# Warm-up on a tile of ones, and sums of squares behind the products, in the opening of an encoder layer

## The chip, the cores and the metric

The kernel runs on one core of a Trainium2 chip. The metric is the device time of one execution in microseconds (us), the median over timed runs. Before the change it is 1359.25 us (three runs, 1358.98 to 1361.77).

The core's engines each run their own queue of instructions in order: TensorE (PE, matmuls), VectorE (DVE), ScalarE (ACT), GpSimd (POOL) and SyncE (SP, which here only issues DMAs). They wait for one another through semaphores. A DMA that is to write into a buffer still in use stands at the head of its queue until the buffer is free, and what was queued after it stands too.

## The reference, cut to what matters

One layer of a bidirectional encoder: sequence 1024, model width 1024, fp32. Only the beginning matters here.

```python
cond = jax.nn.silu(c)
mod = cond @ w_ada[l] + b_ada[l]
sh1, sc1, g1, sh2, sc2, g2 = jnp.split(mod, 6, axis=-1)
h = modulate(rms_norm(x, norm_mix_g[l]), sh1, sc1)      # (x * rsqrt(mean(x*x)) * g) * (1 + sc1) + sh1
proj = h @ w_in[l]
q_a, k_a, v_a, qk_m, v_m, o_m, gates = jnp.split(proj, splits, axis=-1)
...                                                      # attention and mLSTM heads, output projection, SwiGLU
```

The sum of squares of each of the 1024 tokens is needed for the norm, but the norm is a factor per token and can be multiplied in after a projection.

## The kernel before

Everything is held transposed: x is eight tiles of 128 model rows by 1024 tokens (`x_t[k]`, k = 0 to 7), worked on in two halves of 512 tokens (n = 0, 1). A product in fp32 quality is made from three fast ones: both operands are split into a rounded high part and a remainder (`hh` and `hl` for the input, `whi` and `wlo` for weights), and `mm3` (line 311) issues high x high, high x low and low x high. ACT makes the high part, DVE or POOL the remainder. A plain fp32 matmul (the warm-up, the sums of squares) is two passes on PE.

**The opening.** While x and the first rows of w_ada arrive, DVE makes a column of `mod` from each ada tile (`ada_load`, line 565, 512 KB each, a tile ring of five; a8 to a15 give the scale sc1, a0 to a7 the shift). `z_steps` (line 570) scales x by sc1 and splits it, before the norm is known. PE then runs, for each k, the products of that k with three column tiles of w_in (f = 0, 1, 2) into six PSUM accumulators `acc0` (the loop at line 700). The weights come in pieces of four k: pieces 0 to 2 serve k = 0 to 3 and pieces 3 to 5 the rest; `split` (line 461) splits each after its DMA into a ring of three `wst` tiles.

**The sums of squares.** `square_steps` (line 547) has ACT square each half of each x_t. For k below `PES` (3) the square is a tile of `small()` (line 519, a ring of five) that PE adds up over the 128 rows with a matmul by `ones`, into `msp[n]` (line 704). From k = 3 on DVE adds the squares into `ssx`, and after k = 5 one more matmul per half adds that (line 720). In the old order the two sums of a k stand ahead of its products.

**After k = 5** `rstd_steps` (line 616) makes the reciprocal root of each half: a root on ACT and a scaled copy on DVE, a square on ACT, and two steps on DVE. Then `h_steps` (line 686), for each n and k, multiplies x by it (DVE), applies scale and shift (ACT, needs column k of the shift), rounds (ACT) and takes the remainder (POOL, or DVE for the first): new `hh` and `hl`. Up to three such chains are open at a time (`last[-3:-2]`). The three sums of `acc0` are read by DVE at the same time, times the root; when all six are read, the flag `late` is set, which the DVE steps of a4 to a7 wait for. After the eighth shift column ACT makes a diagonal matrix of the shift (`diagonal`, line 659). The next products (`acct`, from line 2128) use the new `hh` and `hl`, one k after the other.

**What sets the order.** All instructions are written out under a manual schedule by a planner (`Clock`, line 127) at the time the program is built. It keeps a clock for PE (`ck.t`), estimated free times of the other engines and a heap of events; a `chain` is a row of steps, each of which is written out when the planner's time reaches the end of the step before. `ck.need` moves PE's planned time to that of a flag, `ck.pe(d)` moves it by d, and both write out all events up to then. So a change of PE's planned time changes how instructions of other engines interleave in their queues, though the engines on the chip run by their real waits. The warm-up matmuls are not counted by the planner. The loads at the start follow a list (line 590: x tiles, ada tiles and weight pieces), and each is written out 5 us before the planner's DMA clock reaches it (line 604). Outside that list, three more weight pieces are loaded behind the products of k = 3:

```python
            z_read[k].set(ck, ck.t)
            if k == 3:
                for _ in range(3):
                    load_piece()
```

`load_piece` (line 488) issues the DMA on SP and appends the two steps of the split to ACT's and DVE's queues for the time when the planner has the piece arrive. Nearly all DMAs of the opening go through `dma` (line 316) to SP's queue.

## Time and profile before

| | us |
|---|---|
| timed runs, median of 3 | 1359.25 (1358.98 to 1361.77) |
| profiled execution, its own time | 1354.44 |
| profiled execution, span of its instructions | 1352.7 |
| PE busy | 1275.2 (94%) |
| DVE busy | 1053.8 (78%) |
| ACT busy | 710.0 (52%) |
| POOL busy | 533.6 (39%) |
| first PE instruction | 7.26 |
| warm-up matmuls (line 684) | 7.29 to 12.3 |

The times within the profile count from the span's first instruction. A row of a list gives start, duration, engine, line, operation, written and read tile by their names (buffer numbers left out), shape and count; a bracket gives the engine's idle time before it and what ended it. Line 98 is the wrapper through which all DVE, ACT and POOL steps are written out, so those steps are told apart by their tiles. Line 317 likewise stands for nearly all DMAs. PEld is the loading of the stationary operand, which overlaps the matmuls; matmuls are pipelined, so their spacing is read from starts, not from durations.

### The profile page before, as it was taken

How to read it: one execution, taken by the hardware profiler on the slowest of the kernel's cores; microseconds unless marked ns; L12 is line 12 of the kernel's file. 1: busy time of each engine (PE TensorE's matmuls, PEld its weight loads, DVE VectorE, ACT ScalarE, POOL GpSimd, SP SyncE). 2: the span in 40 equal slices, each digit the busy share in tenths (PEclk: the TensorE clock that was granted, in tenths of full speed). 3: DMA queues.
4: the chain of work that ended last, by engine and by line, in shares of the span. 5: the costliest groups of instructions: out<-in, count | busy, mean ns of one | idle time of the engine just before them, and what ended most of it. 6: DMA issues, size and time to landing. Idle time of an engine off the chain costs nothing.

```text
span 1352.7 us, 19570 instructions
## 1 busy us (share of the span) xinstructions
PE 1275.2 (94%) x6596; PEld 1072.6 (79%) x6596; DVE 1053.8 (78%) x1683; ACT 710.0 (52%) x1342; POOL 533.6 (39%) x454
## 2 busy tenths in 40 slices
PE   7898888899999989999999999999999999999997
PEld 5777767788778979788778788888888887788886
DVE  7936698976789847889888989876666655888886
ACT  6576366778577756455477522333232333554452
POOL 0352577655666523444125155555544530000002
PEclk9898999999999999999999999999999999999999
DMA  9444332233233226673553344423332258943324
GB/s 365 158 138 131 107 110 94 88 99 108 66 93 106 75 83 199 216 263 113 179 179 113 101 144 145 137 94 109 110 117 86 72 178 304 335 109 94 94 58 161
DMA packets 104468, 187.02 MB, mean 138 GB/s; under 512 B 11568, under 2 KB 33200, under 8 KB 104368
## 3 DMA queue, kind: packets, MB, share of 16 engines
q1 hardware_dynamic: 90976, 163.68, 38.0%
q10 hardware_dynamic: 13392, 22.10, 4.3%
q8 instruction: 52, 0.85, 0.2%
q14 instruction: 48, 0.39, 0.1%
HBM read 139.33 MB, written 42.73 MB: 135 GB/s over the span
## 4 chain that ended last, share of the span: by engine, by line
PE 61%; DVE 18%; issue 7%; DMA 5%; ACT 5%; POOL 3%; SPq 1%; DVEq 0%; ACTq 0%; POOLq 0%
PE acc L314 16%; PE acc L312 16%; PE acc L313 16%; DVE sst L98 3%; DVE x L98 2%; DVE y L98 2%; PE av L1210 2%; PE T L1191 2%; DVE PT L98 2%; PE S L1159 2%; SPq L317 1%; PE U L1917 1%; DVE wlo L98 1%; POOL wlo L98 1%; PE ni L2001 1%
## 5 line engine op out<-in xcount | busy, mean ns | idle before, releaser
L98 ACT ACTIVATE whi<-wst 128x512 fp32r<-128x512 f32 (+2 forms) x223 | 134.0, 606 | 141.7 <-PE acc L314 60.1
L98 POOL TENSOR_TENSOR wlo<-wst,whi 128x512 fp32r<-128x512 f32 (+1 forms) x83 | 129.6, 1566 | 178.3 <-ACT whi L98 127.4
L313 PE MATMUL acc<-x,whi 128*128 128x512 f32 x352 | 136.9, 389 | 0.0
L98 POOL TENSOR_SCALAR P<-P,sst 128x1024 f32<-128x1024 f32 x64 | 86.0, 1345 | 88.0 <-DVE sst L98 67.0
L98 DVE TENSOR_TENSOR wlo<-wst,whi 128x512 fp32r<-128x512 f32 (+2 forms) x140 | 93.2, 669 | 32.0 <-ACT whi L98 31.4
L312 PE MATMUL acc<-hh,whi 128*128 128x512 f32 x224 | 96.9, 432 | 6.2 <-ACT xp L98 4.7
L98 POOL TENSOR_TENSOR x<-x,ny 128x256 f32<-128x256 f32 (+1 forms) x8 | 8.3, 1066 | 234.7 <-DMA wst<-act_d1T 214.3
L98 POOL TENSOR_TENSOR wlo<-wr,whi 128x512 fp32r<-128x512 f32 x52 | 72.2, 1389 | 71.7 <-ACT whi L98 68.6
L314 PE MATMUL acc<-whi,wcl 128*128 128x512 f32 x244 | 95.3, 390 | 2.6 <-DVE wcl L98 2.6
L312 PE MATMUL acc<-whi,wch 128*128 128x512 f32 x244 | 95.2, 390 | 2.4 <-ACT wch L98 2.4
L98 ACT ACTIVATE P<-S,sst,colq 128x1024 f32<-128x1024 f32 x64 | 77.2, 1207 | 34.4 <-DVE sst L98 30.5
L313 PE MATMUL acc<-wlo,wch 128*128 128x512 f32 x244 | 94.9, 389 | 0.0
L98 DVE TENSOR_TENSOR PT<-T,PT 128x512 fp32r<-128x512 f32 x128 | 83.3, 681 | 9.5 <-ACT PT L98 9.3
L313 PE MATMUL acc<-hl,whi 128*128 128x512 f32 x224 | 90.4, 404 | 0.0
L314 PE MATMUL acc<-hh,wlo 128*128 128x512 f32 x224 | 90.3, 403 | 0.0
L98 ACT ACTIVATE whi<-wr 128x512 fp32r<-128x512 f32 x56 | 35.4, 632 | 100.0 <-DVE wr L98 48.3
L1191 PE MATMUL T<-ident,P 128*128 128x128 f32 x512 | 71.9, 278 | 16.0 <-DVE PT L98 10.9
L98 ACT ACTIVATE PT<-T 128x512 fp32r<-128x512 f32 x128 | 71.8, 597 | 27.7 <-PE T L1191 26.9
L98 DVE TENSOR_REDUCE sst<-S 128x1 f32<-128x1024 f32 x64 | 77.7, 1213 | 9.8 <-PE S L1159 9.5
L312 PE MATMUL acct<-whi,hh 128*128 128x256 f32 (+1 forms) x256 | 80.5, 314 | 4.6 <-ACT hh L98 3.2
L1191 PEld LDWEIGHTS T<-ident,P 128*128 128x128 f32 x512 | 58.4, 142 | 27.3 <-issue 10.6
L1210 PE MATMUL av<-PT,va 128*128 128x256 f32 x512 | 70.9, 285 | 7.1 <-DVE PT L98 7.0
(482 smaller groups left out, 3855.0 us busy)
## 6 DMA issues: line engine op xcount, KB each, us to landing
wr<-in_w_gu_dram SPq DMA_DIRECT2D x66, 256.0 KB, 2.8
ada<-in_w_ada_dram SPq DMA_DIRECT2D x64, 256.0 KB, 3.4
wd<-in_w_d_dram SPq DMA_DIRECT2D x22, 512.0 KB, 6.8
wst<-in_w_gu_dram SPq DMA_DIRECT2D x42, 256.0 KB, 3.0
wst<-act_d SPq DMA_DIRECT2D x33, 256.0 KB, 3.1
ada<-in_w_ada_dram SPq DMA_DIRECT2D x16, 512.0 KB, 6.9
wst<-in_w_o_dram SPq DMA_DIRECT2D x32, 256.0 KB, 3.5
act_d<-sg ACTq DMA_DIRECT2D x29, 256.0 KB, 2.0
```

Source lines behind the costliest of these rows:

```text
L98: return fn(*args, **kw)
L312: nc.tensor.matmul(acc, w[0], x[0], start=first, stop=False)
L313: nc.tensor.matmul(acc, w[0], x[1], start=False, stop=False)
L314: nc.tensor.matmul(acc, w[1], x[0], start=False, stop=last)
L317: (q or nc.sync).dma_start(dst, src)
L1159: nc.tensor.matmul(sp[:, halves(n)], qs[:, j * P:(j + 1) * P], k2[g][m][:, halves(n)], start=m == 0, stop=m == 1)
L1191: nc.tensor.transpose(tp[:, k], Pt[q][:, (4 * b + k) * P:(4 * b + k + 1) * P], ident)
L1210: nc.tensor.matmul(av, va[:, k, h // 4], PT[it][m][:, k], start=(k, m) == (0, 0), stop=(k, m) == (NJ - 1, 1))
L1917: nc.tensor.matmul(U, T[:, i], wv[:, i], start=True, stop=True)
L2001: nc.tensor.matmul(ni, x["q"][:, i * P:(i + 1) * P], H["Cs"][b][:, i4], start=True, stop=True)
```

## The change

Two edits. The warm-up becomes 34 matmuls of the tile `ones` by itself, 128 columns wide, into the first 128 columns of the same accumulator; they read no input. And the two sums of squares of k = 0, 1 and 2 are written out after that k's products rather than ahead of them; the waits of the planner (`ck.need`, `ck.pe`) move with them.

```diff
-WARM = 4
+WARM = 34
...
         for _ in range(WARM):
-            nc.tensor.matmul(acc0[0][0][0], ones, x_t[0][:, 0:HALF], start=True, stop=True)
+            nc.tensor.matmul(acc0[0][0][0][:, 0:P], ones, ones, start=True, stop=True)
...
         for k in range(KT):
-            if k < PES:
-                for n in range(NH):
-                    ck.need(sq_ok[k][n])
-                    nc.tensor.matmul(msp[n][0], ones, by_pe[k, n], start=k == 0, stop=False)
-                    ck.pe(0.86)
             for n in range(NH):
                 ck.need(z_ok[k][n])
                 for f in range(3):
                     mm3(acc0[f][n][0], weights([f, 3 + f], k, 4), (h_hi[k][:, halves(n)], h_lo[k][:, halves(n)]),
                         k == 0, k == KT - 1)
                     ck.pe(0.68)
+            if k < PES:
+                for n in range(NH):
+                    ck.need(sq_ok[k][n])
+                    nc.tensor.matmul(msp[n][0], ones, by_pe[k, n], start=k == 0, stop=False)
+                    ck.pe(0.86)
             z_read[k].set(ck, ck.t)
```

## The prediction

> **What bounds the kernel now.** I read the page first, then the time-ordered list of each engine over the opening, then busy time by stretch. Over the whole span TensorE (PE) is the bound:

> ```profile
> PE 1275.2 (94%) x6596; PEld 1072.6 (79%) x6596; DVE 1053.8 (78%) x1683; ACT 710.0 (52%) x1342; POOL 533.6 (39%) x454
> ```

> The change lies in the first 44 us, so that stretch has to be read by itself. PE's list there and shortly after (start, duration, engine, line, operation, in brackets the idle time before it and who ended it):

> ```profile
> 7.29 5.19 PE L684 MATMUL acc<-x,ones 128*128 128x512 f32 x8 [7.29 <-DMA x<-in_xT_dram]
> 12.31 1.88 PE L704 MATMUL ms<-sq,ones 128*128 128x512 f32 x4
> ...
> 18.18 1.88 PE L704 MATMUL ms<-sq,ones 128*128 128x512 f32 x4
> ...
> 24.00 1.88 PE L704 MATMUL ms<-sq,ones 128*128 128x512 f32 x4
> ...
> 29.81 0.39 PE L312 MATMUL acc<-hh,whi 128*128 128x512 f32 x1
> ...
> 53.41 0.39 PE L312 MATMUL acct<-whi,hh 128*128 128x272 f32 x1 [1.30 <-ACT hh L98]
> ...
> 56.54 0.60 PE L314 MATMUL acct<-whi,hl 128*128 128x272 f32 x1 [2.61 <-DVE hl L98]
> ...
> 72.15 0.39 PE L312 MATMUL acct<-whi,hh 128*128 128x272 f32 x1 [1.95 <-ACT hh L98]
> ...
> 73.50 0.39 PE L314 MATMUL acct<-whi,hl 128*128 128x272 f32 x1 [0.83 <-POOL hl L98]
> ```

> The list is to be read by its brackets. PE sits idle for 7.29 us until x0 has landed, then runs four warm-up matmuls (5.19), k=0's two sums of squares (L704), k=0's products, and so on; no row from there to 51.9 has an idle bracket. After that it waits four times, for ACT, DVE and GpSimd (POOL). What the other engines were doing meanwhile:

> ```profile
> 29.82:42.06 12.24, 12.24 (x55) 10.13 (x54) 12.18 (x23) 6.54 (x11) 0.00 (x0) 1.00 0.83 288
> 42.06:52.00 9.94, 9.94 (x41) 7.33 (x39) 9.94 (x18) 6.16 (x13) 0.00 (x0) 1.00 0.70 242
> ```

> The columns are the stretch's length, then busy time of PE, weight loads, DVE, ACT and POOL, the granted clock and the DMA. VectorE (DVE) is full too: 12.18 of 12.24 us and 9.94 of 9.94. The waits from 53 to 73 end on hh and hl, the rewritten inputs, whose first step is a product on DVE. So DVE's queue sets the end of the opening, and PE's arriving sooner is worth little as long as that queue has no hole.

> **Part 1, the warm-up.** Eight passes (four fp32 matmuls, two passes each) go, 68 passes of 128 columns come. They need only the tile of ones, which is set by 1.1 us. Their pace, from weight loads, one per pass:

> ```profile
> 9.98 0.34 PEld L684 LDWEIGHTS acc<-x,ones 128*128 128x128 f32 x1 [0.52 <-issue]
> 10.60 0.19 PEld L684 LDWEIGHTS acc<-x,ones 128*128 128x128 f32 x1 [0.28 <-issue]
> ...
> 97.03 1.75 PEld L784 LDWEIGHTS ms<-con,sqk 128*128 128x128 f32 x15 [0.24 <-issue]
> ```

> A load and the idle time before it are one pass of 512 columns: 0.34 + 0.52 = 0.86 us at 9.98, and 0.43 from 10.60 on (0.19 + 0.24 in its neighbours). The pace changes some 3.1 us after PE's start. 128 columns are a quarter: 0.21 slow, 0.107 fast; and the last row, fifteen short passes with a load each in 1.75 us, 0.11 a pass, shows that loading does not hold that pace up. So 3.1 us hold 15 slow passes, the other 53 take 5.7, and the warm-up ends near 1.1 + 3.1 + 5.7 = 9.9. That is the lower end. If each pass also paid its load of 0.19 in full, 68 x 0.19 + 3.1 + 1.1 puts the end at 17. I take 9.9, since the row of fifteen does the same thing. When can products start?

> ```profile
> 11.24 1.42 DVE L98 SCALAR_TENSOR_TENSOR hl<-x,sc,hh 128x512 fp32r<-128x512 f32 x2
> 12.57 1.29 DVE L98 TENSOR_TENSOR wlo<-wst,whi 128x512 fp32r<-128x512 f32 x2
> ```

> A product of k=2 takes (29.81 - 24.00 - 1.72) / 18 = 0.227. The first remainder hl of k=0 is there at 12, the last weight tile at 12.57 + 1.29 = 13.86. So the first half's nine products, which need them one by one, end near 14.2, and the other nine at 16.25. Before, they ended at 18.18: 1.93 sooner.

> **Part 2, the sums after the products.** Two sums are four passes of 0.43, 1.72. Before, k=0's filled the time in which the weights were being split; now they come behind the products. Counting on from 16.25: sums 17.97, k=1 22.05, sums 23.8, k=2 27.9, sums 29.61. At the start of k=3 the changed PE has done the same work at 29.61 as the old one at 29.82: a gain of 0.21, and L720 comes 0.21 sooner. DVE's full queue hides it; I count 0. Without that cover it is worth 0.21.

> The sums free the squares' tiles, a ring of five. The sixth square (k=2, second half) must wait for k=0's first sum, now done near 16.25 + 0.86 = 17.1:

> ```profile
> 17.26 0.62 ACT L98 ACTIVATE sq<-x 128x512 f32<-128x512 f32 x1
> ...
> 19.50 1.34 ACT L98 ACTIVATE hh<-x,sc 128x512 fp32r<-128x512 f32 x2 [0.36 <-DVE sc L98]
> ```

> It just fits: cost 0. If the warm-up ended at 17, k=0's products would end near 21.1 and this square would stand until 22, with hh of k=2 behind it on ScalarE (ACT) and hl behind that on DVE; ACT's idle 0.36 taken off, some 4.4 would reach DVE: the upper bound of this part.

> **Part 3, the order.** The planner in the kernel writes the instructions out by a clock of its own. That clock decides their order, and I use it for nothing else. It counts 0.86 for a sum and 0.68 for three products. In the old plan k=0's sums hid in the wait for the first split; now every sum adds to PE's planned time. The products of k=1 and k=2 begin at the same planned moments as before (16.90 and 22.70), where sums used to go first; those of k=3 begin 2 x 0.86 later, 28.50 against 26.78, and end at 32.58 instead of 30.86. Right there three weight pieces are loaded (lines 713 to 715). Loads of ada come in the plan every 1.456 (512 KB at the planner's 360 GB/s): a3 at 29.65, a4 at 31.10, a5 at 32.56. So the pieces, which stood ahead of a4, now fall behind a5, by 0.02. The queue of SyncE (SP), which issues in order:

> ```profile
> 21.22 13.09 SPq L317 DMA_DIRECT2D ada<-in_w_ada_dram  x6
> 34.40 0.39 SPq L317 DMA_DIRECT2D wst<-in_w_t_dram  x1
> 35.73 0.33 SPq L317 DMA_DIRECT2D ada<-in_w_ada_dram  x1
> 36.15 0.38 SPq L317 DMA_DIRECT2D wst<-in_w_f_dram  x1
> 36.63 0.38 SPq L317 DMA_DIRECT2D wst<-in_w_t_dram  x1
> 41.74 2.62 SPq L317 DMA_DIRECT2D ada<-in_w_ada_dram  x3
> ```

> a5 stands at 41.74 for its buffer (five tiles; it takes a0's, which DVE frees at 41.6). Three pieces now issue behind it, at about 42.2, 42.6 and 43.0 instead of 34.4 to 36.6. Their landing, and what is queued behind:

> ```profile
> DMA to landing us min/median/max: 3.4/5.0/8.5
> ```
> ```profile
> 39.38 0.64 ACT L98 ACTIVATE whi<-wst 128x544 fp32r<-128x544 f32 x1
> 43.18 0.69 ACT L98 ACTIVATE sq<-ms,both 128x512 f32<-128x512 f32 x1 [3.16 <-PE ms L720]
> ```
> ```profile
> 45.70 1.28 DVE L98 TENSOR_SCALAR sq<-ms 128x512 f32<-128x512 f32 x2
> ...
> 50.54 1.29 DVE L98 TENSOR_TENSOR x<-x,sq 128x512 f32<-128x512 f32 x2
> ...
> 58.80 1.22 DVE L98 SCALAR_TENSOR_TENSOR ada<-ada,cond 128x1024 f32<-128x1024 f32 x1
> ...
> 66.71 1.87 DVE L98 TENSOR_TENSOR x<-x,ms 128x512 f32<-128x512 f32 x3
> ```

> In the new plan the first split (41.43) still precedes the first root (41.70, the row at 43.18) on ACT. So ACT would wait for the piece's DMA until 42.2 + 3.5 = 45.7; I take nearly the lowest landing, since the DMA (the last but one figure, 0.21) is nearly idle before:

> ```profile
> 41.00:42.00 1.00, 1.00 (x6) 0.84 (x5) 1.00 (x3) 0.00 (x0) 0.00 (x0) 1.00 0.21 82
> ```

> Behind that wait stand both roots, two more splits, the squares of the roots and four small steps: some 4.3 us of ACT by such rows, to 50.0; on DVE both halves' last two steps then take until 51.8, where x0's product starts instead of at 50.54. That is **+1.3**, with bounds +0.5 (DVE's steps slip in between) and +6.3 (a landing of 8.5).

> One step gains by the same shift. DVE's old order is x0 to x4, four ada steps (58.80), then x5 to x7 (66.71). The ada steps wait for PE's sums to be read, in the plan 0.4 later (55.08 against 54.66), while x5 stays at 54.97: it now goes ahead. On ACT, x5 no longer stands behind the diagonal:

> ```profile
> 67.02 2.44 ACT L98 ACTIVATE diag<-ident,mod 128x128 f32<-128x128 f32 x8
> 69.37 2.21 ACT L98 ACTIVATE x<-x,mod,sc 128x512 f32<-128x512 f32 x3
> ```

> PE's stop at 73.50 (k=5) becomes one at k=6, a block of 2.3 us further on, and ACT has one step of 0.7 less before it. The diagonal is later by 1.3 and by x5's 0.6 on DVE. Sum at 80 us, when PE has finished this loop: +1.3 + 0.6 - 0.7 - 2.3 = **-1.1** (bounds -1.9 and +3.9).

> **After that** the plan is the old one with small exchanges I cannot follow. The next large wait:

> ```profile
> 104.76 1.12 PE L777 MATMUL ms<-sqk,con 128*128 128x512 f32 x2 [3.04 <-DVE sq L98]
> ```

> It can swallow the 1.1 or vanish (3.0): I carry -1.1 through, with -3 and +3 as ends. The profiled execution took 1354.44 around a span of 1352.7 and would take 1353.3; the timed runs lie 4.8 higher, at 1359.25, which gives **1358.2**.

> **The rivals.** (a) Faster: the new order falls well, the late pieces cost only 0.5 (sum -1.9) and two thirds of the wait at 104.76 go too (-2): 1355.3. For it: PE waits 1.30 + 2.61 + 1.95 + 0.83 = 6.7 between 52 and 74, all on queues whose order changes. Against it: DVE has no room from 30 to 52.
> (b) Slower: the late pieces. They share the DMA engines with a5 to a7, and some landing takes the 8.5 of the row. From a landing above 7.3 us the delay exceeds 2.4 + 2.7 and shows; at 8.5 the sum is +3.9: 1363.2. Against it: little else is being moved around 41, so a short landing is likelier.
> (c) The ring: a warm-up that ends late or a cold clock holds the sixth square. The stretch 52 to 60 has PE at half pace after waits of 1.30 and 2.61:

> ```profile
> 52.00:60.00 8.00, 4.08 (x16) 3.57 (x16) 8.00 (x13) 6.17 (x11) 5.34 (x4) 0.67 0.00 0
> ```

> Between a warm-up's end at 9.9 and the first products near 11 to 12 lie 1 to 2 us, then there are holes until 13.9. If the clock (0.67 granted there) fell likewise, ten products at 0.43 cost 2.1, the sum 0.8 more, the square is 2.8 late, 2.4 of it reach DVE: 1360.6. [...]
> (d) That PE gains what it seems to: the 1.93 of k=0 survives to the end. Part 2's count speaks against it; it would be 1357.3, no different to the clock.

> **How the numbers follow.** 0.2% is 2.7 us, about what a measurement of this kernel can tell from no change. Forecast with (d): 0.42. (c): 0.06, also within it. (a): 0.30, faster. (b): 0.22, slower. So faster 0.30, same 0.48, slower 0.22. The range reaches into (a) by the -3 end of the later waits (1359.25 - 1.9 - 3 = 1354.4) and to (b)'s 1363.2.

> **What would show it.** Right: warm-up from about 1.2 to 10; sums at 16 to 18, k=3 near 29.6; SP issues a5 before three pieces, at 42; ACT idle before a split until about 45.7; x5 before the ada steps on DVE. Wrong: pieces still issued at 34 to 37 (then the opening is unchanged to 0.2 us), ACT's sixth square waiting for L704, or L312 at 0.43 a product near 12.

## The result, and the profile after

| | before | after |
|---|---|---|
| median of the timed runs, same chip | 1358.98 (7 runs) | 1348.1 (7 runs) |
| profiled execution, span | 1352.7 | 1346.3 |
| mean granted clock | 0.985 | 0.988 |

The two medians lie 10.9 us apart; the ratio on record, which is not the quotient of the medians, is 0.9945, 95% interval [0.9925, 0.9965]: 7.5 us faster, within 4.8 and 10.2. The forecast was 1358.2, with 1354.4 and 1363.2 as its ends, and no measurable change as the likeliest outcome. That was 1.1 us in the right direction; the size and the place were missed, although the opening ended within the bounds given for it.

**The opening.** PE's list of the changed kernel (start, duration, engine, line, operation, idle time before it):

```profile
1.12 10.03 PE L684 MATMUL acc<-ones 128*128 128x128 f32 x68 [1.12 <-DVE ones L284]
11.62 0.49 PE L312 MATMUL acc<-hh,whi 128*128 128x512 f32 x1 [0.47 <-ACT hh L98]
...
16.82 1.88 PE L710 MATMUL ms<-sq,ones 128*128 128x512 f32 x4
...
28.46 1.88 PE L710 MATMUL ms<-sq,ones 128*128 128x512 f32 x4
29.78 0.79 PE L312 MATMUL acc<-hh,whi 128*128 128x512 f32 x1
```
```profile
56.97 0.59 PE L312 MATMUL acct<-whi,hh 128*128 128x272 f32 x1 [4.49 <-ACT hh L98]
58.50 0.60 PE L314 MATMUL acct<-whi,hl 128*128 128x272 f32 x1 [0.70 <-DVE hl L98]
```

k=3 starts at 29.78, against 29.81 before: what the early products win, the sums behind them take back. The new loop starts at 56.97 instead of 53.41, and the waits of 1.95 and 0.83 us that stood at 72 are gone. SP, ACT and DVE show why:

```profile
22.45 20.75 SPq L317 DMA_DIRECT2D ada<-in_w_ada_dram  x8
43.28 0.38 SPq L317 DMA_DIRECT2D wst<-in_w_t_dram  x1
```
```profile
47.36 0.66 ACT L98 ACTIVATE whi<-wst 128x544 fp32r<-128x544 f32 x1 [3.05 <-DMA wst<-in_w_t_dram]
```
```profile
54.16 1.29 DVE L98 TENSOR_TENSOR x<-x,sq 128x512 f32<-128x512 f32 x2
...
60.16 1.87 DVE L98 TENSOR_TENSOR x<-x,ms 128x512 f32<-128x512 f32 x3
61.95 1.28 DVE L98 SCALAR_TENSOR_TENSOR ada<-ada,cond 128x1024 f32<-128x1024 f32 x1
```

The weight pieces fell behind a5, ACT stood for the first of them until 47.36, and x0's product came at 54.16 instead of 50.54. Then x3 to x5 went in one row ahead of the ada steps, which won 2.6 us back.

**After the opening.** I cut both traces at the same PE instructions and compared what lies between (us; the first two columns are the times of before at the cuts):

| from | to | before | after | difference |
|---|---|---|---|---|
| 0 | 53.4 | 53.4 | 57.0 | +3.6 |
| 53.4 | 80.0 | 26.6 | 24.0 | -2.6 |
| 80.0 | 200.0 | 120.0 | 120.2 | +0.2 |
| 200 | 240 | 40.0 | 38.3 | -1.7 |
| 240 | 400 | 160.0 | 159.9 | -0.1 |
| 400 | 450 | 50.0 | 48.4 | -1.6 |
| 450 | 520 | 70.0 | 71.7 | +1.7 |
| 520 | 575 | 55.2 | 53.2 | -2.0 |
| 575 | 660 | 84.8 | 84.8 | -0.1 |
| 660 | 760 | 100.0 | 98.6 | -1.4 |
| 760 | 1134.8 | 374.8 | 374.5 | -0.3 |
| 1134.8 | 1165 | 30.2 | 28.5 | -1.7 |
| 1165 | 1352.7 | 187.7 | 187.2 | -0.4 |

At 80 us the changed kernel is 1.0 *behind*. It gains in stretches where its program is, instruction for instruction on every queue, the old one: the written orders differ only up to some 105 us. Four waits of PE in before (the bracket is the wait), at 220, 404, 554 and 751 us:

```profile
224.44 0.63 PE L1191 MATMUL T<-ident,P 128*128 128x128 f32 x4 [3.42 <-POOL P L98]
406.12 0.93 PE L1191 MATMUL T<-ident,P 128*128 128x128 f32 x4 [2.00 <-DVE PT L98]
556.45 1.17 PE L2001 MATMUL ni<-Cs,mq 128*128 128x260 f32 x2 [2.21 <-DVE num L98]
753.77 0.50 PE L314 MATMUL acc<-h220h,wlo 128*128 128x512 f32 x1 [2.75 <-DVE wlo L98]
```

Busy time by stretch shows what differs there. Of before, four pairs: the 3.41 us in which such a wait ends, and the 3.41 us behind them (length, busy time of PE, weight loads, DVE, ACT, POOL with their instructions, granted clock, DMA):

```profile
221.98:225.40 3.42, 0.96 (x7) 0.91 (x8) 3.42 (x5) 1.36 (x2) 3.32 (x3) 1.00 0.08 19
225.40:228.81 3.41, 3.41 (x12) 2.73 (x11) 2.56 (x4) 2.69 (x6) 1.62 (x2) 0.50 0.43 154
402.89:406.30 3.41, 1.41 (x8) 0.89 (x7) 3.41 (x10) 1.04 (x2) 0.28 (x1) 1.00 0.00 0
406.30:409.72 3.42, 3.42 (x13) 2.93 (x12) 3.38 (x6) 2.33 (x4) 0.00 (x0) 0.50 0.73 232
553.08:556.49 3.41, 1.20 (x11) 1.02 (x10) 3.38 (x9) 0.39 (x1) 1.60 (x2) 1.00 0.66 197
556.49:559.90 3.41, 3.41 (x13) 3.06 (x14) 2.01 (x7) 0.91 (x4) 0.00 (x0) 0.50 0.30 74
751.05:754.46 3.41, 0.69 (x3) 0.61 (x4) 3.41 (x7) 3.13 (x7) 0.00 (x0) 1.00 0.00 0
754.46:757.88 3.42, 3.42 (x10) 2.67 (x9) 3.42 (x7) 1.40 (x3) 0.00 (x0) 0.50 0.20 77
```

And the changed kernel around the same four waits, cut on its own grid:

```profile
220.75:224.17 3.42, 2.13 (x10) 1.25 (x8) 2.74 (x5) 3.09 (x8) 3.34 (x2) 1.00 0.00 0
224.17:227.58 3.41, 2.70 (x16) 2.38 (x17) 3.37 (x6) 1.87 (x3) 3.31 (x3) 1.00 0.35 96
401.66:405.07 3.41, 1.83 (x10) 1.20 (x7) 3.41 (x9) 1.62 (x4) 0.88 (x1) 1.00 0.01 2
405.07:408.49 3.42, 3.00 (x18) 2.60 (x19) 3.38 (x6) 1.74 (x3) 0.00 (x0) 1.00 0.54 188
551.85:555.26 3.41, 1.89 (x15) 1.62 (x13) 3.38 (x7) 0.39 (x1) 2.32 (x2) 1.00 0.55 192
555.26:558.67 3.41, 2.73 (x20) 2.61 (x20) 2.81 (x11) 1.51 (x6) 0.00 (x0) 1.00 0.19 50
746.41:749.82 3.41, 1.98 (x9) 1.14 (x7) 3.41 (x7) 2.67 (x5) 0.00 (x0) 1.00 0.00 0
749.82:753.23 3.41, 2.08 (x9) 1.75 (x10) 3.41 (x7) 2.69 (x5) 0.00 (x0) 1.00 0.03 11
```

The records of the granted clock, from 10.36 us on in before and from 5.71 us on in after, change on a grid of 3.41 us alone: each of their half-clock stretches ahead of 1300 us is 3.41 or 6.83 us long, one window of that grid or two. In before, the waits at 404 and 554 us lie inside one window, the one at 751 all but 0.03 us of it, and the one at 220 all but its first 0.96 us; PE is busy for 0.69 to 1.41 us of that window, and the next one runs at 0.50. In after the three later waits (2.0, 2.2 and 2.75 us) are as long as before, but a window's edge cuts each of them, and the first has become two of 1.0 us; PE has at least 1.83 us of work in each of these windows, more than half, and the clock stays at 1.00. Between 200 and 1300 us the trace of before shows six half-clock windows, these four and two at 505 us; after has two, at 504 and 511.

So the four rows of the table that hold these waits make -6.7 us. The row from 450 to 520 takes 1.7 back: there before has its two half-clock windows side by side, and after has two with a full one between them. The row from 1134.8 to 1165 is another matter: neither trace has a half-clock window in it. PE waits there for the split of weights, twice in before and once in after, while the share of the DMA engines stands at 1.04 (1152 to 1156 us in before):

```profile
1152.58 0.50 PE L312 MATMUL acc<-whi,wch 128*128 128x512 f32 x1 [0.97 <-ACT wch L98]
1155.34 0.50 PE L314 MATMUL acc<-whi,wcl 128*128 128x512 f32 x1 [2.02 <-DVE wcl L98]
```
```profile
1149.41 0.50 PE L314 MATMUL acc<-whi,wcl 128*128 128x512 f32 x1 [1.55 <-DVE wcl L98]
```

Why they differ is open. In three other profiles of the experiments below that have no half-clock window there either, the row gives +0.2 (`warm_only`), -1.2 (`pe_order_only`) and -1.7 (`sums_only`, which has the old warm-up), so its 1.7 is not counted as the change's.

### The profile page after: what moved, and what is told of

Same layout as the page of the kernel before. It is cut to its first block, busy times and chain, and to the rows that moved or that the text cites. A ratio compares the mean times of both kernels' runs of the same rounds, so it can differ in the third digit from the quotient of the medians.

```text
span 1346.3 us, 19691 instructions
## 1 busy us (share of the span) xinstructions
PE 1275.8 (95%) x6656; PEld 1076.8 (80%) x6656; DVE 1053.4 (78%) x1683; ACT 709.6 (53%) x1342; POOL 537.6 (40%) x454
## 4 chain that ended last, share of the span: by engine, by line
PE 62%; DVE 20%; DMA 6%; ACT 5%; issue 4%; POOL 2%; SPq 1%; ACTq 0%; DVEq 0%; POOLq 0%
PE acc L312 17%; PE acc L314 17%; PE acc L313 17%; DVE sst L98 3%; DVE x L98 3%; DVE y L98 3%; DVE PT L98 2%; PE av L1210 2%; PE T L1191 2%; DVE ada L98 1%; PE S L1159 1%; DMA wst<-act_d 1%; ACT P L98 1%; DVE wlo L98 1%; PE ni L2001 1%
## 5 line engine op out<-in xcount | busy, mean ns | idle before, releaser
L98 ACT ACTIVATE whi<-wst 128x512 fp32r<-128x512 f32 (+2 forms) x223 | 134.0, 606 | 145.0 <-PE acc L314 61.0
L98 POOL TENSOR_TENSOR wlo<-wst,whi 128x512 fp32r<-128x512 f32 (+1 forms) x83 | 130.1, 1573 | 174.8 <-ACT whi L98 126.2
L98 POOL TENSOR_SCALAR P<-P,sst 128x1024 f32<-128x1024 f32 x64 | 85.9, 1343 | 85.5 <-DVE sst L98 64.2
L98 DVE TENSOR_TENSOR wlo<-wst,whi 128x512 fp32r<-128x512 f32 (+2 forms) x140 | 92.3, 663 | 30.6 <-ACT whi L98 30.1
L312 PE MATMUL acc<-hh,whi 128*128 128x512 f32 x224 | 96.3, 430 | 8.4 <-ACT xp L98 6.4
L98 POOL TENSOR_TENSOR x<-x,ny 128x256 f32<-128x256 f32 (+1 forms) x8 | 8.3, 1068 | 232.3 <-PE acc L314 212.3
L98 POOL TENSOR_TENSOR wlo<-wr,whi 128x512 fp32r<-128x512 f32 x52 | 72.3, 1389 | 71.5 <-ACT whi L98 68.4
L314 PE MATMUL acc<-whi,wcl 128*128 128x512 f32 x244 | 95.3, 390 | 2.2 <-DVE wcl L98 2.2
L312 PE MATMUL acc<-whi,wch 128*128 128x512 f32 x244 | 95.0, 390 | 1.2 <-ACT wch L98 1.2
L98 ACT ACTIVATE P<-S,sst,colq 128x1024 f32<-128x1024 f32 x64 | 77.2, 1206 | 31.9 <-DVE sst L98 26.9
L98 DVE TENSOR_TENSOR PT<-T,PT 128x512 fp32r<-128x512 f32 x128 | 83.4, 681 | 9.4 <-ACT PT L98 9.2
L314 PE MATMUL acc<-hh,wlo 128*128 128x512 f32 x224 | 89.3, 399 | 0.1
L98 ACT ACTIVATE whi<-wr 128x512 fp32r<-128x512 f32 x56 | 35.3, 632 | 99.1 <-DVE wr L98 48.3
L312 PE MATMUL acct<-whi,hh 128*128 128x256 f32 (+1 forms) x256 | 81.4, 318 | 5.8 <-ACT hh L98 4.5
L98 ACT ACTIVATE PT<-T 128x512 fp32r<-128x512 f32 x128 | 71.7, 595 | 27.7 <-PE T L1191 26.9
L98 DVE TENSOR_REDUCE sst<-S 128x1 f32<-128x1024 f32 x64 | 77.6, 1213 | 7.6 <-PE S L1159 7.5
L98 POOL TENSOR_TENSOR ada<-ada,cond 128x512 f32<-128x512 f32 x48 | 72.2, 1507 | 20.5 <-DMA ada<-in_w_ada_dram 20.2
```

Source lines behind the costliest of these rows:

```text
L98: return fn(*args, **kw)
L312: nc.tensor.matmul(acc, w[0], x[0], start=first, stop=False)
L314: nc.tensor.matmul(acc, w[1], x[0], start=False, stop=last)
```

## The experiments

All ratios are to before, timed on the same chip beside it. "Windows" says behind which of the four waits (220, 404, 554, 751 us) the profiled execution shows a half-clock window.

| label | PE starts at | windows behind | median | ratio, 95% interval |
|---|---|---|---|---|
| before | 7.3 | 220 404 554 751 | | 1 |
| b_again | 7.6 | 220 404 554 751 | 1355.87 | 0.9994 [0.9977, 1.0010] |
| a_again | 1.1 | 404 | 1351.50 | 0.9957 [0.9943, 0.9972] |
| pe_order_only | 1.1 | 751 | 1350.99 | 0.9949 [0.9930, 0.9968] |
| queue_order_only | 7.5 | 220 404 554 751 | 1356.82 | 0.9998 [0.9981, 1.0014] |
| warm_only | 1.1 | 554 751 | 1353.06 | 0.9967 [0.9953, 0.9981] |
| sums_only | 7.6 | 220 404 554 751 | 1355.12 | 0.9993 [0.9979, 1.0006] |
| late17 | 9.8 | 220 404 554 | 1359.50 | 1.0018 [1.0003, 1.0033] |
| late34 | 13.7 | none | 1363.20 | 1.0041 [1.0024, 1.0059] |
| before_fill4 | 7.6 | none | 1350.85 | 0.9956 [0.9939, 0.9973] |
| after_fill3 | 1.1 | none | 1349.94 | 0.9957 [0.9941, 0.9974] |
| after_more | 1.2 | 220 | 1352.70 | 0.9970 [0.9951, 0.9989] |
| before_more | 7.6 | none | 1354.89 | 0.9992 [0.9974, 1.0010] |
| before_fillC | 7.5 | 554 751 | 1353.81 | 0.9971 [0.9953, 0.9989] |
| before_fillDEF | 7.4 | 220 | 1353.41 | 0.9968 [0.9954, 0.9982] |
| pieces_fill | 1.1 | none | 1354.03 | 0.9977 [0.9962, 0.9992] |

Medians are those of 6 to 12 executions, the windows those of a single one; the two needn't agree to the microsecond. Before's own median was 1356.3 to 1357.6 beside them.

### PE's order or the other queues' order

Both kernels again, unchanged, and the change taken apart. `pe_order_only` has PE's instructions of after, with the planner's clock moved as before, so that ACT, DVE, POOL and SP keep their old order; `queue_order_only` the reverse:

```diff
 # pe_order_only, against after: the planner counts the sums at their old place
+            if k < PES:
+                for n in range(NH):
+                    ck.need(sq_ok[k][n])
+                    ck.pe(0.86)
             for n in range(NH):
 ...
                     nc.tensor.matmul(msp[n][0], ones, by_pe[k, n], start=k == 0, stop=False)
-                    ck.pe(0.86)
```
```diff
 # queue_order_only, against before: the planner counts the sums behind the products
                     nc.tensor.matmul(msp[n][0], ones, by_pe[k, n], start=k == 0, stop=False)
-                    ck.pe(0.86)
 ...
                     ck.pe(0.68)
+            if k < PES:
+                ck.pe(0.86)
+                ck.pe(0.86)
```

> The kernel before, unchanged, so that its granted clock is known run by run (the one profile of it has 0.985, 44 us at half clock; the one of the changed kernel 0.988, 35 us). If the 0.55% come from the number of half-clock windows (3.41 us each) that an execution happens to meet, the ratio here is 1.000, the runs spread over 6 us or more, and the time falls by about 0.6 us for each us of clock lost; at equal clock loss the kernel before is then within 2 us of the changed one. If they come from the order of the queues or from PE's order, the kernel before stays some 4 to 8 us above the changed one at equal clock loss.

> The changed kernel once more on the same chip as the others. Ratio 0.9945 as before if the gain belongs to the kernel; nearer to 0.998 if the seven runs shown were lucky in their clock windows.

> The warm-up on ones and the sums behind the products on PE, with the planner's clock kept as before, so that ACT, DVE, POOL and SP have the old order to the instruction. If the new order of those queues makes the gain, this is 1.000 (0.999 to 1.001), with k=3 at 29.6 and x0's product at about 50.5 as before. If the early warm-up or the earlier products make it, this is near 0.995.

> The old PE order and old warm-up, with the planner's clock moved as the change moves it, so that ACT, DVE, POOL and SP have the changed kernel's order to the instruction. If the queue order makes the gain, about 0.995 with the pieces issued at 42 to 43 and x5 ahead of the ada steps. If PE's order makes it, 1.000 or slightly slower, since the late pieces cost 3 us at x0's product.

The gain comes again (0.9957), it belongs to PE's order (0.9949) and not to the queues (0.9998). So all that my Part 3 worked out, the late pieces and x5, comes to nearly nothing: in `queue_order_only` the stretch to 53.4 us grows by 3.3 and the next, to 80 us, shrinks by 2.2.

The expectation of `b_again` asked for more: whether the time goes by the clock that an execution loses (its span times what its mean granted clock lacks to 1). On this chip before lost 24.0 us on average, `a_again` 20.2 and `pe_order_only` 18.0. With one slope for before and `a_again`, an execution is 0.57 us longer per us lost, and at equal loss before is still 3.7 us (standard error 0.7) above `a_again`. That lies between the two answers set out, within 2 us and 4 to 8, and decides nothing by itself.

### Which of the two edits, and when PE starts

`warm_only` and `sums_only` make one edit each. `late17` and `late34` are after with the tile of ones set again and again by DVE, so that PE begins later, and a shorter warm-up:

```diff
-WARM = 34
+WARM = 26        # late34: 18
-    nc.vector.memset(ones, 1.0)
+    for _ in range(13):        # late34: 25
+        nc.vector.memset(ones, 1.0)
```

> The first edit alone: 34 matmuls on ones from 1.1 us, the sums still ahead of the products, all queues but PE as before. Theory 1 (the clock's windows of 3.41 us lie where PE's first work puts them, and a stall of 2 to 3 us slows the clock only when it fills most of one window): gain as in the changed kernel, ratio about 0.995, 36 to 40 us at half clock, none at 225 and 556. Theory 2 (the products' earlier start makes the gain): 1.000, since PE runs the sums first as before and its products start at 14.

> The second edit alone: sums behind products, warm-up of four on x0 from 7.3 us; all queues in the changed kernel's order. Theory 1: ratio 1.000, some 46 to 50 us at half clock, with windows at 225 and 556 as before. Theory 2: about 0.995.

> The changed kernel with the tile of ones set 13 times, so that the warm-up (26 matmuls) starts about 1.7 us, half a window, later and ends as before. Theory 1 with the windows tied to PE's first work: they move by 1.7 against the program, the half-clock windows fall on other stalls, and the time changes by 2 to 6 us, likely upwards. If the windows are tied to nothing in the kernel: 0.9945 to 0.996, like the changed kernel.

> As late17 with 25 settings and 18 matmuls, so that the warm-up starts about 3.4 us, a whole window, later. Theory 1 with windows tied to PE's first work: back to the changed kernel's pattern and time, 0.995. If the windows are tied to nothing in the kernel: the same value, but then late17 has it too.

The early warm-up carries the larger part (0.9967), the moved sums alone nothing (0.9993); together they give 0.9949 to 0.9957, so the sums add some 2 us only behind the early warm-up, which the intervals do not quite separate. `warm_only` fits neither theory: the window behind 220 us goes, the one behind 554 stays. Its executions lost only 1.0 us of clock less than before's (22.0 against 23.0, standard error 1.2) for a mean 4.0 us shorter, so part of its gain has no account here. The late starts, for which both theories had 0.995 or, for `late17`, a change of 2 to 6 us, missed: they came out later than meant (9.8 and 13.7: 12 and 24 more settings of the tile put PE's start off by 8.7 and 12.6 us), and push the whole opening back (by 6.3 and 7.4 at the cut at 80 us); of that, 3.2 and 6.9 us are left at the end. `late34` warns of the method: its profiled execution, which has none of the four windows, took 1358.91 and is the fastest of its seven, whose median is 1363.2.

One theory of these runs falls: that PE's first work sets where the windows lie. Between PE's first instruction and the first full-clock window pass 3.1 (before), 4.6 (after), 3.8 (`a_again`, the same kernel), 5.9 (`late17`) and 5.0 us (`late34`): no fixed time.

### Filling the four waits

If half-clock windows are the gain, before must gain as much when PE is kept busy in the four waits. `fill` adds to the sum that PE has open, directly ahead of the waiting instruction, products of zeros and ones, which change no result (`zero` is a column of zeros set at the start, `CUR[-1]` the tile of the sum begun last; the lines that set them are left out):

```diff
+    def fill(where, acc=None):
+        if acc is None:
+            acc = CUR[-1]        # the PSUM tile of the open sum
+        for _ in range(FILL.pop(where, 0)):
+            nc.tensor.matmul(acc[:, 0:P], zero.to_broadcast([P, P]), ones, start=False, stop=False)
 ...
                     tp, f = psum_tile([P, 4, P], "T")
+                    if b == 0 and ("T", q) in SITES:      # C: query block 9 (220 us), D: 43 (404 us)
+                        fill(SITES["T", q])
                     for k in range(4):
```

E stands likewise ahead of the tenth `ni` (554), F ahead of the third product of the first "22" (751). `before_fill4` has C to F (12, 7, 7, 9 matmuls), `after_fill3` D to F, `before_fillC` C, `before_fillDEF` the other three.

> Before, with short matmuls of zeros by ones added to the sum that TensorE has open, where it stands for 3.42 us (220 us), 2.00 (404), 2.21 (554) and 2.75 us (751): 12, 7, 7 and 9 of them, 0.21 us each, behind which the waiting instruction stands as before. They change no result. In the profiles so far the granted clock falls to half for one window of 3.41 us after each of these four places in before (225.4, 406.3, 556.5, 754.5) and after none of them in after. Theory windows (the gain is that after's stalls fall into the 3.41 us grid so that fewer windows are less than half busy, each such window costing 1.3 to 1.7 us): the four windows go, ratio to before 0.995 to 0.997, which is the whole gain of the change, with its opening as of old. Theory start (something else that the early start moves, of which the windows are only a sign): 0.999 to 1.001, and the stalls stay or grow elsewhere.

> After, with the same matmuls of zeros at 404, 554 and 751 us (7, 7 and 9), where its profile shows no half-clock window. The control for the addition by itself. Both theories: as after, 0.993 to 0.996 of before; theory windows allows up to 1 us less, for the executions in which one of these windows does fall to half (one did in the second profile of after, at 407.7).

> Before with the 12 matmuls of zeros at 220 us alone (the stall of 3.42 us). Theory chain (the half-clock window behind this stall sets where the later stalls of 2.0, 2.2 and 2.75 us fall on the 3.41 us grid, so that without it they fall as in after, where one in four or none brings a window): most of what the four places gave together, ratio 0.995 to 0.997. Theory each for itself: one window, 1.3 to 1.7 us, 0.9985 to 0.9995, and the windows behind 404, 554 and 751 us stay.

> Before with the matmuls of zeros at 404, 554 and 751 us alone (7, 7 and 9), the stall of 3.42 us at 220 us left as it is. Theory each for itself: three windows of 1.3 to 1.7 us go, 0.996 to 0.998, and the window at 225 us stays. Theory chain says the same of this kernel; the two differ in the one with the place at 220 us alone.

PE's list and busy time by stretch of `before_fill4`:

```profile
225.03 2.84 PE L336 MATMUL acc<-ones,both 128*128 128x128 f32 x24
228.60 0.63 PE L1209 MATMUL T<-ident,P 128*128 128x128 f32 x4 [0.73 <-POOL P L99]
```
```profile
223.66:227.08 3.42, 3.42 (x26) 3.15 (x25) 3.42 (x3) 1.26 (x3) 3.32 (x2) 1.00 0.00 0
404.57:407.98 3.41, 3.41 (x24) 2.98 (x22) 3.41 (x10) 1.70 (x4) 0.96 (x1) 1.00 0.01 2
554.76:558.17 3.41, 2.61 (x22) 2.39 (x21) 3.31 (x11) 0.00 (x0) 0.67 (x1) 1.00 0.49 154
749.32:752.73 3.41, 3.39 (x24) 3.01 (x23) 3.41 (x6) 3.07 (x6) 0.00 (x0) 1.00 0.00 0
```

The waiting instruction at 220 us starts as long after the work before it as in before, but for 0.15 us (2.84 + 0.73 in place of 3.42); PE has only worked meanwhile, and none of the four half-clock windows is left. 35 matmuls that compute nothing take 6.7 us off before, with before's opening. That is as much as the change did (0.9956 against 0.9957 for `a_again`), and after with its own waits filled gains nothing on top (0.9957).

The same cuts as in the table above show it place by place. The difference to before's trace, in us; a star marks a half-clock window that is still there:

| stretch of before | 200 to 240 | 400 to 450 | 520 to 575 | 660 to 760 |
|---|---|---|---|---|
| after | -1.7 | -1.6 | -2.0 | -1.4 |
| a_again | -1.7 | 0.0* | -1.9 | -2.2 |
| pe_order_only | -1.7 | -1.5 | -2.0 | -0.1* |
| warm_only | -1.4 | -1.3 | -0.4* | 0.0* |
| late17 | +0.8* | 0.0* | -0.4* | -2.2 |
| before_fill4 | -1.0 | -1.5 | -1.8 | -2.3 |
| before_fillC | -1.6 | -1.4 | -0.4* | +0.5* |
| before_fillDEF | -0.1* | -1.3 | -2.1 | -0.8 |

Over the 16 profiles beside before's, the 23 such stretches with a window are at most 0.4 us shorter than before's, and the 41 without one are 0.5 to 2.4 us shorter, but for one (`before_more`, 200 to 240). So it is shown that the four windows are worth what the change gained, and that its profiles gain where they are missing. That the medians of after owe all of their gain to them is not shown: `a_again` lost 3.8 us of clock less than before for a mean 5.8 us shorter, `before_fill4` 6.2 less for 6.6.

C alone takes 3.7 us, D to F 4.1. By the table one window would be 1.0 to 1.7 and three 4 to 6; C takes D's window along. Of `before_fillC`:

```profile
401.54:404.95 3.41, 2.49 (x16) 1.86 (x13) 3.41 (x10) 1.81 (x4) 1.52 (x2) 1.00 0.01 2
404.95:408.37 3.42, 2.37 (x15) 2.09 (x16) 3.38 (x7) 1.10 (x2) 0.00 (x0) 1.00 0.42 125
551.70:555.10 3.40, 1.21 (x12) 1.03 (x10) 3.37 (x9) 0.39 (x1) 1.60 (x2) 1.00 0.59 197
555.10:558.50 3.40, 3.40 (x13) 3.06 (x14) 2.02 (x7) 0.92 (x4) 0.00 (x0) 0.51 0.31 81
```

D's wait of 2.0 us lies across the edge of the first two rows, at 404.95, and no half clock follows. E's and F's windows stay. So neither theory holds whole: with C filled D's wait lies otherwise on the grid, and E's lies as it did (PE is busy for 1.21 us of its window, 1.20 in before). That the pair of half-clock windows at 505 us (505.29 to 512.12 in before) sets the later places anew is my reading of these two profiles and was not shown; with executions this far apart (12 of each kernel) I don't press the difference of 3.7 from one window's price further.

### More places, and the opening mended

`after_more` and `before_more` are `after_fill3` and `before_fill4` with A (102 us, 12), G (184 us, 6) and B (157 us, 14 matmuls into a spare PSUM tile) filled too. `pieces_fill` is after with C to F filled and the three pieces asked for between the halves of k=3:

```diff
 # pieces_fill, against after
                     ck.pe(0.68)
+                if k == 3 and n == 0:
+                    for _ in range(3):
+                        load_piece()
 ...
-            if k == 3:
-                for _ in range(3):
-                    load_piece()
```

> After, with the matmuls of zeros also at 102.7 us (12, a stall of 3.76 us), 157.6 us (14 of ones by ones into a spare PSUM tile, a stall of 4.16 us) and 184.4 us (6, a stall of 1.89 us). After these three its profile shows 4 half-clock windows (104.7 twice, 162.7, 186.6). Theory windows: 3 to 4 windows fewer, 4 to 6 us less than after, ratio to before 0.989 to 0.992. Theory start: as after, 0.993 to 0.996.

> Before with the matmuls of zeros at all seven places (102, 157, 184, 220, 404, 554, 751 us). Theory windows: 0.990 to 0.993, and within 2 us of after with its places filled, since what is left between the two is only their openings, which the profiles show 1.0 us apart at 80 us. Theory start: 0.998 to 1.001, and the distance of 6 us to after with its places filled stays.

> The changed kernel with its three weight pieces asked for between the two halves of k=3 (so that they stand on the queue of the transfers where they stood before the change, and ACT doesn't wait for them until 47 us) and the matmuls of zeros at 220 (8), 404, 554 and 751 us. DVE's order of the x products is then that of before again. The opening's two effects were 3.6 us later at x0's product and 2.5 us won back between 54 and 80 us, so the opening ends within 1 us of after's; 0.993 to 0.996 of before, no better than after beyond its spread. A version that beats both would show as 0.992 or less.

All three are misses. The windows at 105, 160 and 187 us went, and the stretch from 104.8 to 167.4 hardly shortened for it: 62.1 against before's 62.6 in `before_more`, and 63.5 against after's 61.3 in `after_more`, with a third to less than half of the half-clock time. There PE waits again soon after (1.0 us at 166 and 1.4 us at 170 for the scores in `before_more`), and the slow windows cost little or nothing. Instead `after_more`, which has no fill at 220 us, has a window behind it, and `before_more` has new ones at 321 and 505 us, whose stretches are 2.8 and 2.0 longer; its stretch from 200 to 240 us has lost the window but is no shorter, since PE waits more at 205 and 221 us (0.7 and 1.1). So none of the four windows and yet no gain (0.9992): in these two kernels the fills ahead of 200 us only moved the windows and waits behind them. `pieces_fill` has none of the four windows, and loses by its opening: its first 80 us take 84.2 against 80.0 and 81.0, with four half-clock windows between 57 and 81 us for after's two. The opening was to end within 1 us of after's; it ended 3.2 later. Nothing here beats both `after` and `before_fill4`.

## Why the prediction was wrong

**Where it failed.** "After that the plan is the old one with small exchanges I cannot follow ... I carry -1.1 through, with -3 and +3 as ends." The plan was indeed the old one, and I took an equal program to have equal times: from 80 us to the end the sum has 0, with 3 either way for the wait at 104.76 alone. The profiles show -7.4 there, of which -6.7 fall on the stretches of the four waits. The program's stalls fall on a grid of 3.41 us that lay 0.8 us apart in two executions of one kernel (its first full-clock window 4.6 us behind PE's first instruction in after, 3.8 in `a_again`), and which of them cost a half-clock window went with small shifts: the wait of 2.0 us at 404 us begins 1.23 us behind an edge in before and 1.83 in after, and before alone has a window at half clock behind it. That was no term of the sum, though the row of 52 to 60 us with its 0.67 lay in the prediction: I weighed the clock for the opening alone, as rival (c). The windows could have been counted in the trace of before: four, behind waits of 2.0 to 3.4 us. In the one behind 751 us, up to 757.88, products start every 0.43 us, and every 0.23 after it:

```profile
755.08 0.63 PE L312 MATMUL acc<-h222h,whi 128*128 128x512 f32 x1
755.50 0.63 PE L313 MATMUL acc<-h222l,whi 128*128 128x512 f32 x1
...
758.21 0.40 PE L314 MATMUL acc<-h220h,wlo 128*128 128x512 f32 x1
758.45 0.40 PE L312 MATMUL acc<-h221h,whi 128*128 128x512 f32 x1
```

So it loses some 1.6 of its 3.41 us, and at that price, an estimate, the four make some 6 us that a shift may take away. That is a rival with a price, and the faster side (0.30) would have had more weight and a lower end. What could not be had from it is which way they fall; that the forecast had the direction right, by its -1.1 in the opening, is luck, since the opening came out at +1.0.

**Part 1** was nearly right. The warm-up ended at 11.15, not at 9.9:

```profile
1.10:5.70 4.60, 4.58 (x21) 4.58 (x22) 0.00 (x0) 1.28 (x1) 0.00 (x0) 1.00 0.62 220
5.70:11.20 5.50, 5.46 (x49) 5.26 (x47) 2.33 (x7) 4.66 (x7) 0.00 (x0) 1.00 1.04 389
```

The slow pace lasted 4.6 us, not 3.1 (21 passes of 0.22), the fast one was 0.11 as read from the fifteen short passes. (The clock column, 1.00 in both rows, has no entry before 5.71 us; the pace shows the change.) k=0's products ended at 16.82, not 16.25.

**Part 2** held: k=3 at 29.78 (29.61 counted), the sixth square without a wait, worth 0.

**Part 3** had the mechanism, all of it: pieces behind a5, ACT waiting for the first of them, x5 ahead of the ada steps, the stops at 72 and 73.5 us gone. Its first term was too small: +1.3 was +3.6. Pieces were issued at 43.28, not 42.2, because DVE was 1.1 late by 26 us already (a landing of an ada tile), the landing took 4.1 instead of 3.5, and ACT and DVE took 6.8 from there to x0, not 6.1. The other terms (+0.6, -0.7 and -2.3, together -2.4) measured -2.6. Sum at 80 us +1.0, not -1.1, within the bounds given.

**What stays open.** Why the early start splits the wait at 220 us. In before DVE's step stands beside POOL's longest one there, in after beside a shorter one:

```profile
220.09 3.27 DVE L98 SCALAR_TENSOR_TENSOR y<-xp,vec,y 128x1024 f32<-128x1024 f32 x1
```
```profile
218.04 4.24 POOL L98 TENSOR_TENSOR qs<-qd,qs 64x1024 fp32r<-64x1024 f32 x1
```
```profile
221.60 1.71 DVE L98 SCALAR_TENSOR_TENSOR y<-xp,vec,y 128x1024 f32<-128x1024 f32 x1
```
```profile
219.58 2.65 POOL L98 TENSOR_TENSOR ada<-ada,cond 128x512 f32<-128x512 f32 x1 [1.25 <-DMA ada<-in_w_ada_dram]
222.30 3.24 POOL L98 TENSOR_TENSOR qs<-qd,qs 64x1024 fp32r<-64x1024 f32 x1
```

The first pair is before's, the rest after's. The same step of DVE takes 1.27 with POOL idle (at 214.06 us in before). Here it begins beside a step of POOL each time and ends 1.08 us behind that step's end in before (222.28) and in after (222.23). In before that step is the long `qs`; in after it is the end of `ada`, and `qs` comes next. What holds the step up there no run shows. ACT's part, ahead of POOL's, waited 2.29 us for its DMA in after and 0.50 in before. No run here moved that DMA alone, so that its landing splits PE's wait is argued and not shown. Likewise open is why D, E and F fall on an edge more often in the early-starting kernels: of four such kernels as first profiled (after, a_again, pe_order_only, warm_only) four of twelve of these places have a window, of the five that have a half-clock window behind 220 us (before, b_again, queue_order_only, sums_only, late17), fourteen of fifteen.

## What to carry to other kernels

Where PE sets the pace, list the half-clock windows of the whole trace before you predict, each with its price and the wait ahead of it. Here an edit in the first 44 us moved four of them, 6.7 us in the profiles, and a change of 0.5% that shows up far behind the edit may well be of that kind. The four waits of 2.0 to 3.4 us could be filled, with 35 matmuls that add nothing to the open sum (0.9956); the same was no use where PE waits again soon after (104.8 to 167.4 us, 62.1 against 62.6). And an experiment must hold such windows still, or be repeated until they average out, before a fraction of a per cent is put down to its edit.

## What the runs showed that was not expected

- The windows of 3.41 us ahead of a half clock were not all idle: the one at 402.89 us in before has PE busy for 1.41 us. In before and after, past 60 us, and of windows that ran at full clock themselves: with PE busy for less than 44% of one the next ran at half clock each time (13 windows, PE busy for 0 to 41%); between 44 and 52% one of three was followed by half clock (183.21 us in after, 45%); from 52% on (720 windows) one was, at 112.78 us in before. Over all 17 profiled executions these are 102 of 102, 13 of 38, and of more than 6000 none but that one place, in 12 of the 17. There, in before, PE is busy for 2.96 of 3.41 us, but for 1.95 us with passes of two columns. Behind a window at half clock it is not so plain: of 136 with PE busy for 52% or more, 23 had another behind them (in before the one at 505.29 us, 75%). Of before, PE's list and busy time by stretch:

```profile
114.07 1.95 PE L784 MATMUL ms<-con,sqk 128*128 128x2 f32 x16 [0.45 <-ACT sqk L98]
```
```profile
112.78:116.19 3.41, 2.96 (x21) 2.46 (x20) 3.41 (x8) 3.01 (x5) 1.42 (x2) 1.00 0.15 59
116.19:119.60 3.41, 3.41 (x9) 2.53 (x8) 1.57 (x5) 0.33 (x2) 0.98 (x1) 0.50 0.91 254
```

  So the busy time that the profile shows doesn't tell every half clock. The windows with the 128-column fills (PE busy for 2.61 to 3.42 us in `before_fill4`) had none behind them; whether passes of two columns count for less was not shown, this place being the only one.
- At the four waits a half-clock window went with 1.4 to 2.0 us between before and after, and in most other profiles with 1.3 to 2.4; between 105 and 167 us, where PE soon waits again, with nothing that shows.
- Executions of one and the same kernel differ by 11 us (before, 1350.9 to 1362.31 on one chip), more than the change.
